# The MLP's up projection by seven block products instead of eight, with all block sums of weights built in device memory

## The chip, the cores and the metric

The kernel runs on one core of a Trainium2 chip. The metric is device time in microseconds. The kernel before takes 828.75 us, the median of three runs (828.61 to 828.80). The engines are named as in the profile: PE is TensorE (matrix products; PEld its weight loads), DVE is VectorE, ACT is ScalarE, POOL is GpSimd, SP is SyncE, which here only issues transfers.

## The reference

One encoder layer over x of 512 tokens by 1024, in float32. A token mixer (two kinds of recurrent heads, both directions) and a cross-attention add to x; then comes the part that is changed, a squared-ReLU MLP with 4096 hidden columns, and a final RMSNorm:

```python
def squared_relu_mlp(xn, w_up, w_down):
    return jnp.square(jax.nn.relu(xn @ w_up)) @ w_down

x = x + squared_relu_mlp(rmsnorm(x, norm_mlp[l]), w_up[l], w_down[l])
```

## The kernel before

**Precision.** Every large product runs as three passes: each operand is split into a rounded part (`hi`, made by ScalarE as a copy) and the rest (`lo`, made by VectorE as a subtraction), and hi·hi, hi·lo and lo·hi are added in PSUM (`split_out`, `mm3`).

**Weights.** The host packs the weights into blocks of 128 by 1024 (`wpk`, 512 KB each) in the order of their use. `load` brings a block to an `st` tile on SP's queue (three buffers), `split` makes its `wh` and `wl` (three buffers each); `weights` keeps splits up to two blocks and loads three blocks ahead, at raised priority.

**Stages.** First the input projections with the recurrent heads interleaved as generators (`tick`), then the memory projections, `out`, the query projection `xq` with the attention heads, the attention's output projection `xo`, and then for f = 0 to 3 an up stage (1024 hidden columns) and a down stage of the MLP.

**Products by seven.** `xo` and the four down stages already use a scheme with seven instead of eight block products (P1 to P7): the token halves and the weight blocks are combined by sums, the seven products accumulate in three PSUM banks per token tile (`by_blocks`), and VectorE adds them to the residual `xr`. Sums of weight blocks (names T2, U, T3) are made by `sum_loads` and `add_block`: POOL issues a plain load into SBUF, and then loads that add on arrival. Each product and half g is one "job" with one weight tile; `ahead` splits the tiles up to two jobs ahead.

**Up before.** `proj_d` runs 8 output blocks of 128 columns, each over 8 blocks of the contraction, three passes, 512 tokens wide. The transposed x (`x3T`, made by `turn_two`) is not yet normalised; the row of factors 1/rms (`rrow`) is multiplied in on the result together with the ReLU, so that the first up blocks (`first_two`) run before the norm is known. ScalarE squares, and VectorE and ScalarE make the sums and splits (`e["P1"]` to `e["P7"]`) for the down stage.

**Order.** TensorE's order in the last stages is the program's order. ScalarE, VectorE and the queues are put in order ahead of time by a planner: each engine takes, of what the plan has ready, what stands earliest in the program; `tc.high_priority()` moves a piece ahead. `behind(a, b)` puts a after b on an engine.

Of the kernel before, what the change touches and what calls it, by code (L numbers as in the profile page):

```python
# [10 lines left out]
F32 = mybir.dt.float32  # L11
# [34 lines left out]
def _split_order():  # L46
# [18 lines left out]
    for f in range(4):  # L65
        for j in range(4):
            seq += d("up", 1024 * f + P * j, 1) + d("up", 1024 * f + P * (j + 4), 1)
        seq += [("t", "down", 8 * f + 2 * g + k, 0) for g in range(2) for k in (0, 4)]
        seq += [("t", "down", 8 * f + 2 * g + 4, 512) for g in range(2)]
# [7 lines left out]
NSTREAM = len(SEQ) - 10  # L77
# [3 lines left out]
def trunk(ctx: ExitStack, tc: tile.TileContext, x, mem, wpk, vec, cst, lmask, rmask, rows, out):  # L81
    nc = tc.nc
    big = ctx.enter_context(tc.tile_pool(name="big", bufs=1))
    sb = ctx.enter_context(tc.tile_pool(name="sb", bufs=1))
    psm = ctx.enter_context(tc.tile_pool(name="psm", bufs=4, space=PSUM))
# [163 lines left out]
    def weights(key):  # L249
        i = SIDX[key]  # L250
        with (tc.high_priority() if i > 2 else ExitStack()):
            for n in range(i, i + 3):
                split(n)
            load(i + 3)
        return hl_tiles[i]

# [819 lines left out]
    ORDER = ("P1", "P2", "P6", "P5", "P7", "P3", "P4")  # L1076
    LATE = [(p, g) for p in ORDER[2:] for g in range(2)]
    JOBS = {f: [("P1", 0), ("P2", 0), ("P1", 1), ("P2", 1)] + LATE for f in range(4)}

    JOBS[-1] = [(p, g) for p in ("P1", "P7", "P2", "P5", "P6", "P3", "P4") for g in range(2)]  # L1080
# [5 lines left out]
    def sum_loads(f, names):  # L1086

        parts = {"T2": ((0, 1), (1, 1), (0, 0)), "U": ((0, 1), (0, 0)), "T3": ((0, 1), (1, 1))}
        for nme in names:
            if nme == "T3":  # L1090
                t2 = [G4()[:, :] for _ in range(2)]
            else:
                t = A16()
                t2 = [t[:, g * 1024:g * 1024 + 1024] for g in range(2)]
            for g in range(2):
                sums[f, nme, g] = t2[g]
        return [add_block(sums[f, nme, g], block(f, g, *parts[nme][i]), i > 0)
                for i in range(3) for nme in names for g in range(2) if i < len(parts[nme])]
# [6 lines left out]
    SUMS = {f: {"P6": "T2", "P5": "U", "P7": "T3", "P4": "T2"} for f in range(4)}  # L1105
    SUMS[-1] = {"P6": "T3", "P5": "U", "P7": "T3", "P4": "T3"}

    def job(f, n):

        if n >= len(JOBS[f]):  # L1110
            if f < 3:
                split(SIDX["d", "up", 0, 1024 * (f + 1)] + n - len(JOBS[f]))
            return None
        p, g = JOBS[f][n]
        if p in PLAIN:
            i = block(f, g, *PLAIN[p])
            split(i)
            return hl_tiles[i]
        if (f, n) not in jobs_hl:
# [343 lines left out]
```

## Time and profile before

| | |
|---|---|
| median of 3 runs | 828.75 us |
| profiled execution | 828.9 us, span 826.9 us |
| granted TensorE clock | 0.998 |
| PE / PEld / DVE / ACT / POOL busy | 98% / 82% / 71% / 52% / 9% |
| DMA | 118.9 MB, mean 144 GB/s |
| `xo`'s end and up stage 0 | 485.4 to 536.5 us |
| down stages f = 0 to 3 | start at 536.5, 618.1, 699.7, 781.3 us, 38.1 us each |
| up stages f = 1 to 3 | start at 574.6, 656.2, 737.8 us, 43.5 us each |

The span runs from the first to the last instruction; the profiled execution's own time has 2.0 us around it. Busy time of matmuls is modelled from their starts: a matmul of 512 columns is listed with 0.39 us though the next one starts 0.23 us after it. Lines named L258 are those of the helper `split_out`; L261 to L263 are `mm3`, L1153 to L1155 the products of `by_blocks`, L1102 POOL's transfers, L236 the weight loads.

### The profile page before, as it was taken

The numbers are of one execution on the slowest core, as the hardware profiler recorded it, in microseconds if no ns is written. First come the engines' busy times: TensorE is split into PE (matmuls) and PEld (weight loads), VectorE is DVE, ScalarE is ACT, GpSimd is POOL, SyncE is SP. The second block draws the span as 40 slices with busy tenths as digits, with TensorE's granted clock in tenths as the row PEclk, the third lists the DMA queues.
The fourth block names the chain that finished last, engine by engine and source line by source line (L and its number), as shares of the span: only waits on it lengthen the run. The fifth ranks groups of instructions, "written<-read, shape, count | busy, mean of one in ns | idle before, by whom it ended". The sixth has DMA issues, their size and how long they took to land.

```text
span 826.9 us, 12625 instructions
## 1 busy us (share of the span) xinstructions
PE 813.4 (98%) x4862; PEld 676.1 (82%) x4862; DVE 590.9 (71%) x1046; ACT 431.9 (52%) x771; POOL 77.7 (9%) x131
## 2 busy tenths in 40 slices
PE   8999999999999999999999999999999999999996
PEld 6788778877878988887888888888888888888885
DVE  6568975699479898545668985676668566756685
ACT  5247564545578485345455675443454345434544
POOL 2000000100010000100100004022102210211001
PEclk9999999999999999999999999999999999999999
DMA  7332223322342334532343349969836982798332
GB/s 277 118 120 91 78 79 106 100 89 79 102 128 78 128 128 154 151 98 83 111 119 76 81 128 302 254 171 275 217 102 182 280 211 91 189 290 207 110 70 101
DMA packets 34125, 118.91 MB, mean 144 GB/s; under 512 B 3921, under 2 KB 4049, under 8 KB 34066
## 3 DMA queue, kind: packets, MB, share of 16 engines
q1 hardware_dynamic: 22832, 77.80, 27.5%
q0 software_dynamic: 10944, 39.85, 21.8%
q8 instruction: 38, 0.62, 0.3%
q10 hardware_dynamic: 290, 0.47, 0.1%
q14 instruction: 21, 0.17, 0.1%
HBM read 116.00 MB, written 2.10 MB: 143 GB/s over the span
## 4 chain that ended last, share of the span: by engine, by line
PE 84%; issue 6%; DVE 6%; ACT 2%; DMA 1%; POOL 1%; POOLq 0%; ACTq 0%; DVEq 0%
PE mm L261 17%; PE mm L263 17%; PE mm L262 17%; PE sm L1153 6%; PE sm L1155 6%; PE sm L1154 6%; PE mm L1153 2%; PE mm L1155 2%; PE mm L1154 2%; DVE wl L258 2%; PE sm L827 1%; PE sm L562 1%; PE sm L486 1%; ACT wh L258 1%; DVE t L759 1%
## 5 line engine op out<-in xcount | busy, mean ns | idle before, releaser
L258 ACT ACTIVATE wh<-st 128x1024 fp32r<-128x1024 f32 x131 | 138.7, 1060 | 185.2 <-PE mm L262 117.9
L261 PE MATMUL mm<-xT,wh 128*128 128x512 f32 x544 | 215.3, 396 | 0.0
L258 DVE TENSOR_TENSOR wl<-st,wh 128x1024 fp32r<-128x1024 f32 x131 | 160.1, 1223 | 76.1 <-ACT wh L258 75.6
L263 PE MATMUL mm<-xT,wl 128*128 128x512 f32 x544 | 212.8, 391 | 0.1
L262 PE MATMUL mm<-xT,wh 128*128 128x512 f32 x544 | 212.4, 390 | 0.3 <-DVE xT L975 0.3
L263 PEld LDWEIGHTS mm<-xT,wl 128*128 128x128 f32 x544 | 102.1, 188 | 21.9 <-DVE wl L258 0.3
L262 PEld LDWEIGHTS mm<-xT,wh 128*128 128x128 f32 x544 | 102.3, 188 | 20.8 <-DVE xT L975 0.9
L261 PEld LDWEIGHTS mm<-xT,wh 128*128 128x128 f32 x544 | 102.2, 188 | 20.7 <-ACT wh L258 0.3
L1102 POOL DMA_DIRECT2D as<-in_wpk x52 | 39.6, 763 | 250.2 <-DVE wl L258 162.0
L1342 DVE SCALAR_TENSOR_TENSOR t<-mm,rg 128x512 f32<-128x512 f32 x32 | 22.0, 691 | 52.1 <-PE mm L263 52.0
L1153 PE MATMUL sm<-wh,yT 128*128 128x512 f32 x128 | 49.8, 389 | 0.0
L1154 PE MATMUL sm<-wl,yT 128*128 128x512 f32 x128 | 49.8, 389 | 0.0
L1155 PE MATMUL sm<-wh,yT 128*128 128x512 f32 x128 | 49.8, 389 | 0.0
L258 ACT ACTIVATE wh<-as 128x1024 fp32r<-128x1024 f32 x26 | 27.6, 1062 | 37.0 <-PE sm L1155 23.7
L258 DVE TENSOR_TENSOR wl<-as,wh 128x1024 fp32r<-128x1024 f32 x26 | 31.9, 1226 | 14.0 <-ACT wh L258 14.0
L1153 PE MATMUL sm<-wh,a 128*128 128x512 f32 x84 | 32.9, 391 | 0.0
L1155 PE MATMUL sm<-wh,a 128*128 128x512 f32 x84 | 32.7, 389 | 0.0
L1154 PE MATMUL sm<-wl,a 128*128 128x512 f32 x84 | 32.7, 389 | 0.0
L1285 DVE TENSOR_TENSOR vv<-vv,sm 128x512 f32<-128x512 f32 x48 | 31.0, 681 | 1.7 <-PE sm L1155 1.7
L199 POOL TENSOR_TENSOR tiny<-tiny,misc 128x4 f32<-128x4 f32 (+1 forms) x10 | 9.6, 963 | 201.3 <-DVE tiny L197 136.2
L1155 PEld LDWEIGHTS sm<-wh,yT 128*128 128x128 f32 x128 | 24.0, 188 | 5.0
L1154 PEld LDWEIGHTS sm<-wl,yT 128*128 128x128 f32 x128 | 24.0, 188 | 5.0
(329 smaller groups left out, 1566.8 us busy)
## 6 DMA issues: line engine op xcount, KB each, us to landing
st<-in_wpk SPq DMA_DIRECT2D x131, 512.0 KB, 3.4
as<-in_wpk POOLq DMA_DIRECT2D x52, 512.0 KB, 6.9
gate<-in_wpk POOLq DMA_DIRECT2D x24, 512.0 KB, 7.1
as<-in_x SPq DMA_DIRECT2D x4, 512.0 KB, 6.8
vv<-in_x SPq DMA_DIRECT2D x8, 256.0 KB, 4.0
out<-vv SPq DMA_DIRECT2D x7, 256.0 KB, 2.2
a<-in_mem SPq DMA_DIRECT2D x2, 512.0 KB, 3.7
t<-in_rows SPq DMA_DIRECT2D x2, 256.0 KB, 5.3
```

The costliest lines, as they stand in the source:

```text
L199: gp.tensor_tensor(out=r, in0=ms, in1=nh.to_broadcast([P, w]), op=ALU.pow)
L258: return sc.activation(dst_hi, src, AF.Copy), v.tensor_tensor(out=dst_lo, in0=src, in1=dst_hi.bitcast(F32), op=ALU.subtract)
L261: pe.matmul(ps, lhsT=ah, rhs=bh, start=first, stop=False)
L262: pe.matmul(ps, lhsT=ah, rhs=bl, start=False, stop=False)
L263: pe.matmul(ps, lhsT=al, rhs=bh, start=False, stop=last)
L486: mm = pe.matmul(ps[b * i:b * i + b, z:z + b], lhsT=kc[j][:, w * P + b * i:w * P + b * i + b], rhs=rhs(j, w * P, i), start=True, stop=True)
L1102: return gp.dma_start(out=dst, in_=wpk[idx], **kw)
L1153: pe.matmul(ps, lhsT=ah, rhs=bh, start=new, stop=False, **fl)
L1154: pe.matmul(ps, lhsT=ah, rhs=bl, start=False, stop=False, **fl)
L1155: pe.matmul(ps, lhsT=al, rhs=bh, start=False, stop=end and k == 1, **fl)
L1285: added = v.tensor_tensor(out=z, in0=z, in1=ps, op=ALU.add if sign > 0 else ALU.subtract)
L1342: v.scalar_tensor_tensor(out=y, in0=ps, scalar=0.0, in1=rrow[:, 0:512], op0=ALU.max, op1=ALU.mult)
```

## The change

**Up by seven products.** The new function `up(st)` splits the 1024 by 1024 up product of a stage into blocks of halves: contraction, hidden columns and tokens. Each half g of 256 hidden columns in a block has seven products, 14 jobs a stage, in an order written out in `MORDER`. A job is 2 output tiles by 4 contraction blocks by 3 passes, 256 tokens wide. P1, P6, P7 and P4 add up in one PSUM bank A, P5 and P3 in a bank C, P2 in a bank B; the bank is read out between the products, and `first` to `fourth` make the sums that the down stage needs from the squared results.

**The normalised x.** The products combine halves of x, so these are multiplied by 1/rms beforehand: `flip` transposes and scales by the gain, `rstd_half` and `norm_half` make the factors of one token half, multiply, combine and split. `after_product` puts their TensorE parts between the products. `first_two`, `turn_two` and `rms_row` go.

**Weights.** For each of the eight MLP stages (up and down) and each g the four sums P5, P7, P6 and P4 are built in device memory by `make_forms`: SP fills a form from a weight block or copies one from another form, POOL adds a weight block to it. One or two steps are issued at each `weights` call from the fifth block on, the rest at every third MLP job. In the MLP each job, form or plain block, is one load on SP (`mload`), three to six jobs ahead; the splits stay up to two jobs ahead (`msplit`). The loads with sums into SBUF remain for `xo` alone. The down stages' order of products becomes P1, P5, P2, P6, P3, P7, P4, g by g.

```diff
-NSTREAM = len(SEQ) - 10
+NSTREAM = SIDX["d", "up", 0, 0]
...
+        for _ in range(0 if i < 4 else 1 + i % 2):
+            next(form_steps, None)
         return hl_tiles[i]
...
+            for g in range(2):
+                for p in ("P5", "P7"):
+                    yield lambda: mfill(nc.sync, f[p, g][:, :], st, g, (0, 1))
+            for g in range(2):
+                yield lambda: mfill(gp, f["P5", g][:, :], st, g, (0, 0), True)
+                yield lambda: mfill(gp, f["P7", g][:, :], st, g, (1, 1), True)
+            for src, dst, b in (("P7", "P6", (0, 0)), ("P6", "P4", (1, 0))):
+                for g in range(2):
+                    yield lambda: nc.sync.dma_start(out=f[dst, g][:, :], in_=f[src, g][:, :], max_dma_last_dim=4096)
+                for g in range(2):
+                    yield lambda: mfill(gp, f[dst, g][:, :], st, g, b, True)
+
+        for s0 in range(0, 8, 2):
+            for a, b in zip(steps(s0), steps(s0 + 1)):
+                a()
+                yield 1
+                b()
+                yield 1
...
+    MORDER = [seq("1a 2a 1b 2b 5a 5b 3a 6a 3b 7a 6b 4a 7b 4b")] + [two("P1", "P5", "P2", "P6", "P3", "P7", "P4"),
+              seq("1a 2a 5a 1b 3a 5b 6a 2b 7a 6b 4a 3b 7b 4b")] * 4
...
+    def mahead(n):
+        with tc.high_priority():
+            for m in range(n, n + 3):
+                msplit(m)
+            for m in range(n + 3, n + 7):
+                mload(m)
+        if n % 3 == 0:
+            next(form_steps, None)
+        return mhl[n]
...
+    def norm_half(u):
+
+        ps = smb()
+        for t in range(2):
+            pe.transpose(ps[:, t * P:t * P + P], rt[u][:, t:t + 1].to_broadcast([P, P]), ident)
+        with tc.high_priority():
+            sc.activation(rrow[:, u * 256:u * 256 + 256], ps[:, 0:256], AF.Copy)
+            for p, x in ((("P1", fx[0, 0]), ("P2", fx[0, 1])) if u == 0 else (("P5", sraw[0]),)):
+                for h in range(2):
+                    times_r(x, u, h)
+                    part_split(p, x, h)
+        if u == 0:
+            return
+        d = sraw[0]
+        x1, x3_, x2_, x4 = fx[0, 0], fx[0, 1], fx[1, 0], fx[1, 1]
+        v.tensor_tensor(out=d, in0=d, in1=x1, op=ALU.subtract)
+        v.tensor_tensor(out=x3_, in0=x3_, in1=d, op=ALU.add)
+        split_out(*xf["P3"], x3_)
+        split_out(*xf["P6"], d)
+        for h in range(2):
+            times_r(x2_, 1, h)
+        v.tensor_tensor(out=x1, in0=x1, in1=x2_, op=ALU.subtract)
+        split_out(*xf["P7"], x1)
+        for h in range(2):
+            times_r(x4, 1, h)
+        split_out(*xf["P4"], x4)
...
+    def up(st):
...
+        def square(t, src):
+            sc.activation(t, src, AF.Relu)
+            sc.activation(t, t, AF.Square)
...
+        def first(g):
+            v.tensor_tensor(out=y[3, g], in0=y[2, g], in1=y[3, g], op=ALU.subtract)
+            form("P5", g, y[3, g], A4)
+        def second(g):
+            v.tensor_tensor(out=y[3, g], in0=y[3, g], in1=y[0, g], op=ALU.subtract)
+            form("P6", g, y[3, g], A4)
...
+        for n, (p, g) in enumerate(MORDER[st]):
+            hi, lo = mahead(len(JOBS) * st + n)
...
+            ps = B[g] if p == "P2" else C[g] if p in ("P5", "P3") else A[g]
+            xh, xl = xf[p]
+            for k in range(2):
+                o = ps[:, k * 256:k * 256 + 256]
+                for kt in range(4):
+                    z = slice(k * 512 + kt * P, k * 512 + kt * P + P)
+                    m = slice(kt * 256, kt * 256 + 256)
+                    new = k == kt == 0 and p in ("P1", "P2", "P5")
+                    pe.matmul(o, lhsT=hi[:, z], rhs=xh[:, m], start=new, stop=False, **fl)
+                    pe.matmul(o, lhsT=hi[:, z], rhs=xl[:, m], start=False, stop=False, **fl)
+                    pe.matmul(o, lhsT=lo[:, z], rhs=xh[:, m], start=False, stop=kt == 3, **fl)
+                after_product()
...
+            if p == "P7":
+                v.tensor_tensor(out=y[3, g], in0=y[3, g], in1=ps, op=ALU.subtract)
+                square(y[3, g], y[3, g])
+                form("P4", g, y[3, g], A4)
+            elif p == "P4":
+                y[2, g] = T2()[:, 0:512]
+                square(y[2, g], ps)
+                first(g)
+                if g == 0:
+                    second(g)
+                    third(g)
+                    fourth(g)
```

More of the change, by code (lines that the diff above doesn't have):

```diff
@@ L1104, in trunk, with job @@
     PLAIN = {"P1": (0, 0), "P2": (1, 0), "P3": (1, 1)}
[L1105 to L1114, printed above, removed]
+    SUMS = {"P6": "T3", "P5": "U", "P7": "T3", "P4": "T3"}
+    def job(n):
+        if n >= len(JOBS):
+            return msplit(n - len(JOBS))
+        p, g = JOBS[n]
@@ L1125, in job @@
                     behind(a, b)
-            jobs_hl[f, n] = (hi, lo)
-            if f < 0 and p == "P7":
-                add_block(s_, block(f, g, 0, 0))
+            jobs_hl[n] = (hi, lo)
+            if p == "P7":
+                add_block(s_, block(-1, g, 0, 0))
             if p == "P6":
-                add_block(s_, block(f, g, 1, 0))
-        return jobs_hl[f, n]
+                add_block(s_, block(-1, g, 1, 0))
+        return jobs_hl[n]
+    two = lambda *ps: [(p, g) for p in ps for g in range(2)]
@@ new lines, in trunk, with mload @@
+    seq = lambda s: [("P" + w[0], "ab".index(w[1])) for w in s.split()]
+    MORDER = [seq("1a 2a 1b 2b 5a 5b 3a 6a 3b 7a 6b 4a 7b 4b")] + [two("P1", "P5", "P2", "P6", "P3", "P7", "P4"),
+              seq("1a 2a 5a 1b 3a 5b 6a 2b 7a 6b 4a 3b 7b 4b")] * 4
+    MJ = [(st, p, g) for st in range(8) for p, g in MORDER[st]]
+    mst, mhl, msum = {}, {}, []
+    def mload(n):
+        if n < len(MJ) and n not in mst:
+            st, p, g = MJ[n]
+            mst[n] = T("st", 1024, 3)
+            if p in PLAIN:
+                mfill(nc.sync, mst[n][:, :], st, g, PLAIN[p])
+            else:
+                nc.sync.dma_start(out=mst[n], in_=mforms[st, p, g][:, :], max_dma_last_dim=4096)
@@ L1218, in heads_in, with after_product @@
             drain()
+    later = []
+    def after_product():
+        for w in list(later):
+            w[0] -= 1
+            if w[0] < 0:
+                later.remove(w)
+                w[1]()
+    fx, rt, sraw = {}, {}, [None]
     def add_out(t, c, ps, sign, last):
         z = xr[t, c]
-        last_add[0] = v.tensor_tensor(out=z, in0=z, in1=ps, op=ALU.add if sign > 0 else ALU.subtract)
-        if last:
+        v.tensor_tensor(out=z, in0=z, in1=ps, op=ALU.add if sign > 0 else ALU.subtract)
+        if not last:
+            return
+        with (tc.high_priority() if (t, c) in ((1, 1), (3, 0)) else ExitStack()):
@@ L1303, in add_to @@
         finish(t, r, pieces[t])
-    def first_two():
-        i0 = SIDX["d", "up", 0, 0]
-        for j in range(2):
-            split(i0 + j)
-        w = [hl_tiles[i0 + j] for j in range(2)]
-        for j in range(2, 5):
-            load(i0 + j)
-        two = [mmb(), mmb()]
-        for half in (4, 0):
-            for j in range(2):
-                for k in range(half, half + 4):
-                    z = slice(k * P, k * P + P)
-                    mm3(two[j], w[j][0][:, z], w[j][1][:, z], x3[k][0], x3[k][1], k == 4, k == 3)
-                    if whole and j == 0 and k == 7:
-                        turn_two(*whole.pop(0)[1:])
-                        with tc.high_priority():
-                            behind(split(i0 + 2), last_add[0])
-        rms_row()
-        return two
```

285 lines of the change are left out of this document (174 added, 111 removed).

## The prediction

> **What bounds the kernel now.** I read the page's engine table and chain first, then who waits on TensorE, then TensorE, VectorE and ScalarE by MLP stage. The first rows are the page's:
>
> ```profile
> span 826.9 us, 12625 instructions
> PE 813.4 (98%) x4862; PEld 676.1 (82%) x4862; DVE 590.9 (71%) x1046; ACT 431.9 (52%) x771; POOL 77.7 (9%) x131
> PE 84%; issue 6%; DVE 6%; ACT 2%; DMA 1%; POOL 1%; POOLq 0%; ACTq 0%; DVEq 0%
> ```
>
> The waits of TensorE, longest and last:
>
> ```profile
> PE sm L349 <- DMA cs<-in_cst: 1.3, 1, 1.3
> ...
> PE mm L262 <- DVE wl L258: 0.2, 1, 0.2
> ```
>
> Seven such rows sum to 5.7 us, none in the MLP. So TensorE's instruction stream sets the time, and time can only be lost if it is made to wait. The stretches (columns: length, then busy time of PE, PEld, DVE, ACT, POOL, clock, DMA share, GB/s) are the first 465 us, the seam from the output projection into the MLP, and one up and one down stage:
>
> ```profile
> 20.70:485.40 464.70, 461.66 (x3296) 386.03 (x3296) 344.49 (x692) 259.70 (x532) 21.58 (x41) 1.00 0.35 105
> 485.40:536.54 51.14, 51.14 (x237) 42.46 (x236) 34.54 (x58) 28.11 (x50) 11.16 (x15) 1.00 0.87 245
> 574.62:618.14 43.52, 43.52 (x193) 36.04 (x192) 27.59 (x42) 19.57 (x29) 3.47 (x4) 1.00 0.64 191
> 618.14:656.22 38.08, 38.08 (x169) 31.53 (x168) 27.60 (x35) 17.04 (x18) 8.51 (x12) 1.00 0.78 195
> ```
>
> An up stage is 192 matmuls in 43.52 us, 0.2267 us each; a down stage 168 in 38.08, the same pace. TensorE is gapless; VectorE is at 63% and 72%, ScalarE at 45%.
>
> **Up by seven products: the gain.** Each up stage becomes 14 block products of 24 matmuls, 336 in all, each 256 columns wide. This width stands in the memory projection; the timeline has 22 of them in a row:
>
> ```profile
> 274.71 0.28 PE L263 MATMUL mm<-a,wl 128*128 128x256 f32 x1
> ...
> 277.23 0.28 PE L263 MATMUL mm<-a,wl 128*128 128x256 f32 x1
> ```
>
> 21 steps in 2.52 us: 0.120 us each, not half of 0.2267 (0.113). So 336 x 0.120 = 40.3 against 43.5: 3.2 us a stage, **12.8 us over four**, 1.5%. If halving were exact it would be 21.8; the row excludes that. A product takes 2.88 us.
>
> The Trainium skill's "TensorE: Matmul & The Clock Gate", section "Back-to-back issue gap", gives N/2.4 + 2.5 ns when warm, so 216 and 109 ns, and by it the four stages would save 18.9 us (an estimate from that page). This trace has 227 and 120 ns, 11 ns more on each, so the trace disagrees and decides: more but narrower matmuls pay that extra 144 times more per stage.
>
> **What VectorE and ScalarE get to do.** Rows of one seam up to down, in time order, ScalarE then VectorE:
>
> ```profile
> 618.12 1.06 ACT L258 ACTIVATE wh<-st 128x1024 fp32r<-128x1024 f32 x1 [3.40 <-PE mm L262]
> 619.08 0.62 ACT L1343 ACTIVATE t<-t 128x512 f32<-128x512 f32 x1
> 622.03 1.14 ACT L258 ACTIVATE yT<-t 128x512 fp32r<-128x512 f32 x2
> ```
>
> ```profile
> 618.34 0.69 DVE L1342 SCALAR_TENSOR_TENSOR t<-mm,rg 128x512 f32<-128x512 f32 x1 [3.01 <-PE mm L263]
> 619.21 1.23 DVE L258 TENSOR_TENSOR wl<-st,wh 128x1024 fp32r<-128x1024 f32 x1 [0.17 <-ACT wh L258]
> 620.35 0.42 DVE L1358 TENSOR_TENSOR t<-t,t 128x256 f32<-128x256 f32 x1
> 620.69 0.68 DVE L258 TENSOR_TENSOR a<-t,a 128x512 fp32r<-128x512 f32 x1
> 621.29 0.42 DVE L1359 TENSOR_TENSOR t<-t,t 128x256 f32<-128x256 f32 x1
> 621.63 0.42 DVE L1360 TENSOR_TENSOR t<-t 128x256 f32<-128x256 f32 x1
> 621.96 0.42 DVE L1361 TENSOR_TENSOR t<-t,t 128x256 f32<-128x256 f32 x1
> 622.30 1.22 DVE L258 TENSOR_TENSOR wl<-st,wh 128x1024 fp32r<-128x1024 f32 x1
> 623.43 1.28 DVE L258 TENSOR_TENSOR yT<-t,yT 128x512 fp32r<-128x512 f32 x2
> ```
>
> Start to start in a full queue, a weight split costs ScalarE 0.96 (618.12 to 619.08) and VectorE 1.13 (622.30 to 623.43); a 512-wide operation costs about 0.57 and 0.60 (620.69 to 621.29). An up stage now has 14 weight splits instead of 8; per half g three bank copies, four squarings of two ScalarE operations each, three subtractions or adds from a bank, and sums and splits for its forms, 11 splits and 5 sums of them within the stage. ScalarE: 14 x 0.96 + (6 + 16 + 11) x 0.57 = 32 us of 40.3 (80%). VectorE: 14 x 1.13 + (6 + 5 + 11) x 0.60 = 29 us (72%). That fits on average. What counts is where TensorE waits for one of these.
>
> **Place one, 7b to 4b.** P1, P6, P7 and P4 accumulate in one bank per g, each read out before the next writes. Everywhere in the orders another product lies between, 2.88 us of cover, except at "7b 4b": 4b may not start until VectorE has subtracted bank A of 7b. With VectorE free that is 0.16 (a matmul's tail, 0.28 less 0.12) + 0.68 + hand-overs of about 0.05: 0.9 us. But 4a ended two products earlier, and releases a chain for g=0: two squarings, then four sums and four splits (VectorE 8 x 0.60), which stand earlier in the program than 7b's subtraction. Beside them lie the sum and split from 3b (1.2) and three weight splits at raised priority (3.4). The sums partly serialise, since the second rewrites in place what P5's split still reads. 9.4 us of VectorE work thus stands ahead of the subtraction, begins about 1.2 us after 4a and has 5.8 us until 7b ends: 1.2 + 9.4 - 5.8 = 4.8 us late. VectorE's order is fixed ahead of the run; that the earlier instruction in the program wins when ready is seen at 620.69, where the split of a (earlier in the code) goes ahead of L1359 to L1361, and at 622.30, where the raised weight split overtakes yT. Bounds 0.9 and 5.9 (with idle gaps while it waits for ScalarE); near the serial case I take **4.0 us, three times: +12**.
>
> **Place two, the seam into up(0).** Before, the first up blocks ran on raw x while the normalisation caught up: 485.40 to 536.54 is gapless. Now the normalised x must be multiplied by r, combined and split before each product. VectorE: P1 and P2 8 x 0.60, P5 6 x 0.60, the rest 2 x 1.2 (scalings) + 7 x 1.13 = 10.3; 18.7 us on top of 29, against 40.3 plus some 3 us of lead. ScalarE: transposed copies and splits, some 12 us on 32. Up to the third pair (3a, 17.3 us into the stage) VectorE owes 23 us of raised splits, adds and forms in about 24 us, with idle gaps while r goes through POOL:
>
> ```profile
> L1261 POOL TENSOR_TENSOR tiny<-tiny,misc 128x4 f32<-128x4 f32 x1 | 1.0, 1032 | 21.0 <-DVE tiny L981 21.0
> ...
> L955 ACT ACTIVATE t<-vv 128x512 f32<-128x512 f32 x24 | 15.0, 626 | 10.3 <-DVE vv L961 5.9 <-DVE vv L1285 3.1 <-DVE vv L1222 1.2
> ...
> L1285 DVE TENSOR_TENSOR vv<-vv,sm 128x512 f32<-128x512 f32 x48 | 31.0, 681 | 1.7 <-PE sm L1155 1.7
> ```
>
> The chain add 0.68, square 0.8 (0.63 and reading its sum), two small steps 0.3, this power 1.0, broadcast 0.4, scale 0.6, split 1.3 is 5 us; cover is the last product of the output projection (5.4 us with its transposes). So P1a and P2a start 0.5 to 1.5 us late, P3 1 to 2, and at "4a 7b 4b", with one product of cover less than later, 7b's subtraction comes 1 to 6 late. Bounds 2 and 12; I take **+7**. The transposes themselves are as many as before.
>
> **Forms in device memory.** Removed: 64 POOL loads into SBUF in the MLP; no TensorE wait named one, so 0. Added: 64 fills and copies on SP's queue, 64 accumulates on POOL's; 97 of the 128 within the 65 weight fetches before the output projection, the rest in the MLP.
>
> ```profile
> q1 hardware_dynamic: 22832, 77.80, 27.5%
> q0 software_dynamic: 10944, 39.85, 21.8%
> st<-in_wpk SPq DMA_DIRECT2D x131, 512.0 KB, 3.4
> as<-in_wpk POOLq DMA_DIRECT2D x52, 512.0 KB, 6.9
> SPq L236 <- DVE wl L258: 483.3, 83, 18.5
> ```
>
> A plain 0.52 MB takes the 16 engines 1.5 us (227 us for 77.8 MB), one of q0's 76 transfers 2.4 on average (180/76). 97 steps at 1.5 to 2.9 us are 145 to 280 us in 465, on a DMA share of 0.35: 0.66 to 0.95. Copies memory to memory stand in no row; a copy waits for an accumulate's landing, and SP's weight loads queue behind it, as POOL's powers do behind an accumulate. But SP already sits waiting for a free buffer 483 us in all: loads run two blocks (11 us) ahead of need, more than 6.9, and each copy comes four steps (over 15 us) behind what it needs. Bounds 0 and +8 (one wait of under 0.1 us per step); I take 0. In the MLP one 0.5 MB load per 2.8 us is 187 GB/s, below 245 reached. The end (P3 now ahead of P7, then P4) is the same length.
>
> Sum: 828.9 (span 826.9 + 2.0 around it; median of the runs 828.75) - 12.8 + 12 + 7 + 0 = **835**.
>
> **Rivals.** *VectorE keeps up* (0.40): 7b's subtraction fits into a gap while VectorE waits for ScalarE, as the 3.0 us idle ahead of 618.34 shows it has gaps today; up(0) loses 3. 828.9 - 12.8 + 3 x 1.1 + 3 = 822. For it: averages of 72 to 80%. Against: the burst sits just there.
>
> *The seams cost little, but the early stages slow down* (0.11): copies on SP meet late accumulates, weight loads come after their need, and TensorE waits where it now waits 5.7 us in all. 822 + 8 to 20: 830 to 842. It decides once a load lands more than 11 us after its slot came free. This is also how the change would not do what it says: forms not ahead of their stage.
>
> *The clock drops* (0.07): after each gap of 4 to 6 us matmuls restart at a lower clock. Here no gap exceeds 1.3 us and the granted clock is 1.00 in every stretch, so no row prices it: 0 at least; if each of four gaps were followed by half pace for as long as the gap itself, 4.5 us, that is 4 x 2.25 = 9 us on the forecast, 844. The Trainium skill's "TensorE: Matmul & The Clock Gate", section "Why this matters for your kernels", asks for no idle gap over about 3 us, or the clock falls back to half; no run here shows it yet.
>
> **Numbers.** Forecast 0.42 (own range 830 to 842), rivals as given. Under 820 or over 846 about 0.15 stays out, so 820 to 846. 0.2%, about what can be told from no change, is 1.7 us. Faster 0.39 (nearly all of the first rival), within 0.2% 0.09, slower 0.52 (the forecast, the clock, most of the second rival).
>
> **What would show it.** Up stages at 336 matmuls with 0.120 us steps; TensorE waits "<- DVE" at the subtraction of P7's bank, three or four of 3 to 5 us, and several around the first up stage; VectorE's queue full there; no waits for weight splits before 480 us. Wrong if those waits are about 1 us (then 822), or if TensorE waits for DMA or weight splits in the early stages.

## The result and the profile after

The changed kernel takes 995.4 us (median of four runs, 994.2 to 998.5) against 828.8 for the kernel before: 1.202 times, interval 1.199 to 1.204. The forecast was 835, its range 820 to 846. The sign was right; 166.6 us were lost where 6.1 were forecast.

The page of the kernel after, its first rows, the clock and DMA slices (40 equal slices of 24.8 us, in tenths), POOL's queue and the longest TensorE waits by place:

```profile
span 993.7 us, 14157 instructions
PE 841.6 (85%) x5438; PEld 722.5 (73%) x5438; DVE 622.1 (63%) x1033; ACT 486.1 (49%) x854; POOL 90.7 (9%) x132
PEclk9985987967597899999999999899999999999998
DMA  9999999999999234334432534245455455465543
q0 software_dynamic: 15040, 39.85, 21.4%
```

```profile
PE sm L647 <- DVE t L640: 26.1, 3, 25.1
PE sm L532 <- DVE a L623: 24.3, 5, 9.3
PE sm L724 <- DVE a L721: 18.7, 1, 18.7
PE sm L588 <- ACT as L580: 18.4, 2, 11.2
PE sm L1497 <- ACT a L304: 16.7, 3, 5.6
```

Four of these five rows lie in the recurrent heads, long before the MLP; before, seven waits summed to 5.7 us. The DMA engines are full for the first 13 slices, and in these the clock is at its lowest (digit 5 in two of them). The stretches of the kernel after (length, then busy time of PE, PEld, DVE, ACT, POOL, clock, DMA share, GB/s):

```profile
20.70:100.00 79.30, 54.16 (x218) 42.60 (x216) 31.77 (x76) 19.45 (x26) 16.90 (x24) 0.81 1.04 274
100.00:200.00 100.00, 76.59 (x760) 60.94 (x760) 47.45 (x88) 35.21 (x55) 20.93 (x24) 0.89 1.06 276
200.00:300.00 100.00, 49.56 (x392) 41.48 (x393) 30.87 (x51) 23.34 (x50) 22.41 (x27) 0.71 1.05 269
300.00:400.00 100.00, 84.59 (x684) 68.94 (x683) 68.81 (x122) 54.25 (x117) 8.38 (x22) 0.91 0.46 128
```

The table gives the stages, read from the timelines as the start of the first matmul of each, in us. The time is the median of the runs; the stages are of the one profiled execution (for e15 its fastest, 829.2). Rows after the second are experiments, told below.

| kernel | time | up f=0 starts | up f=0 | down f=0 | up f=1 | down f=1 |
|---|---|---|---|---|---|---|
| before | 828.8 | 491.6 | 44.9 | 38.1 | 43.5 | 38.1 |
| after | 995.4 | 632.3 | 49.5 | 43.4 | 48.0 | 38.7 |
| e2, no forms | 853.3 | 492.7 | 49.1 | 43.4 | 47.8 | 38.8 |
| e3, and subtraction first | 836.1 | 492.5 | 49.1 | 43.4 | 42.0 | 38.8 |
| e11, and 7b 4a 4b | 835.0 | 492.2 | 48.5 | 43.5 | 40.3 | 40.4 |
| e12, and P2 ahead of P5 | 826.5 | 492.4 | 48.3 | 38.8 | 40.3 | 38.8 |
| e15, all of it with forms | 831.8 | 494.0 | 48.4 | 38.8 | 40.3 | 38.7 |

So the 166.6 us fall into two parts: 140.7 are lost before the MLP begins (632.3 against 491.6), and the other 25.9 after that.

**Ahead of the MLP.** The rows of the form transfers in the kernel after (accumulates, fills, copies: durations of the issue, then first and last start), and of the weight loads issued from 60 to 300 us with the time to their landing:

```profile
L273 POOL DMA_DIRECT2D form_P<-in_wpk x64: 827/1036/1211, 18.1 to 312.5; - x64
L273 SPq DMA_DIRECT2D form_P<-in_wpk x32: 490/597/3691, 12.5 to 255.1; - x32
L290 SPq DMA_DIRECT2D form_P<-form_P x32: 469/470/482, 34.1 to 303.6; - x32
...
L237 SPq DMA_DIRECT2D st<-in_wpk x19: 333/540/1996, 68.0 to 284.5; - x19
DMA to landing us min/median/max: 8.2/12.4/26.4
```

All 128 are gone by 312 us, also the 31 that the program issues in the MLP. Nothing held them to their place: a fill depends on nothing, so the planner, which gives an idle queue whatever is ready, put them ahead. The weight loads came late. The first 28 of them, in the kernel after up to 303.6 us:

```profile
L237 SPq DMA_DIRECT2D st<-in_wpk x28: 328/524/1996, 1.2 to 284.5; - x28
```

The first 28 of the kernel before, and its loads from 60 to 300 us with their landing:

```profile
L236 SPq DMA_DIRECT2D st<-in_wpk x28: 327/328/493, 1.2 to 155.0; - x28
...
L236 SPq DMA_DIRECT2D st<-in_wpk x38: 327/328/336, 60.2 to 299.7; - x38
DMA to landing us min/median/max: 3.0/3.3/4.2
```

The 28th was issued at 284.5 instead of 155.0 us, 129.5 later. From 60 to 300 us there were 19 loads where 38 had been, and one took 12.4 us to land instead of 3.3. Up to 320 us ScalarE waited 14 times, 121.6 us in all, to split a block that had not landed:

```profile
ACT wh L304 <- DMA st<-in_wpk: 121.6, 14, 15.6
```

The longest wait of TensorE came another way. The factor 1/rms of a recurrent head is a power on POOL; what it needs is ready at 238.7 us, but seven accumulates stand ahead of it on POOL's queue, and each of them waits for a transfer to land:

```profile
270.44 1.04 POOL L273 DMA_DIRECT2D form_P<-in_wpk  x1 [7.06 <-DMA form_P<-in_wpk]
271.02 1.53 POOL L200 TENSOR_TENSOR tiny<-tiny,misc 128x4 f32<-128x4 f32 x1
272.59 0.69 DVE L640 TENSOR_TENSOR t<-t,tiny 128x512 f32<-128x512 f32 x1 [33.89 <-POOL tiny L200]
273.43 1.09 PE L647 MATMUL sm<-cs,t 128*128 128x128 f32 x4 [25.08 <-DVE t L640]
```

In the 18.7 us of L724 the last 5.3 are of the same kind: VectorE waits for a memset on POOL behind an accumulate. By these rows some 30 of the 140.7 us come through POOL's queue, and the rest, as far as rows show it, through late weight loads and the clock behind the waits. No run takes POOL's steps alone out of that queue.

**In the MLP.** TensorE's first matmul of 4b in up f=1 and VectorE's queue ahead of it:

```profile
768.43 0.55 PE L1497 MATMUL sm<-xT,wh 128*128 128x256 f32 x1 [5.58 <-ACT a L304]
```

```profile
762.84 0.69 DVE L1469 TENSOR_TENSOR t<-t,as 128x512 f32<-128x512 f32 x1
...
764.05 0.68 DVE L1473 TENSOR_TENSOR rg<-rg,t 128x512 f32<-128x512 f32 x1
764.66 1.22 DVE L304 TENSOR_TENSOR wl<-st,wh 128x1024 fp32r<-128x1024 f32 x1
...
767.00 0.68 DVE L1477 TENSOR_TENSOR as<-as,t 128x512 f32<-128x512 f32 x1
767.60 0.68 DVE L1520 TENSOR_TENSOR t<-t,sm 128x512 f32<-128x512 f32 x1
```

L1469, L1473 and L1477 are `second`, `third` and `fourth` of half 0; L1520 is the subtraction from P7's bank. It ends at 768.28 and TensorE starts at 768.43. The releaser that the row names (a form's split on ScalarE) is not the one: raised in e3, the subtraction takes most of the gap away. After the gap comes the clock:

```profile
768.40:772.00 3.60, 3.57 (x17) 3.60 (x18) 1.36 (x2) 1.81 (x3) 0.00 (x0) 0.50 0.11 40
```

### The profile page after: what moved, and what is told of

Its sections match the earlier page's. It is cut to its first block, busy times and chain, and to the rows that moved or that the text cites. A ratio compares the mean times of both kernels' runs of the same rounds, so it can differ in the third digit from the quotient of the medians.

```text
span 993.7 us, 14157 instructions
## 1 busy us (share of the span) xinstructions
PE 841.6 (85%) x5438; PEld 722.5 (73%) x5438; DVE 622.1 (63%) x1033; ACT 486.1 (49%) x854; POOL 90.7 (9%) x132
## 3 DMA queue, kind: packets, MB, share of 16 engines
q0 software_dynamic: 15040, 39.85, 21.4%
## 5 line engine op out<-in xcount | busy, mean ns | idle before, releaser
L304 DVE TENSOR_TENSOR wl<-st,wh 128x1024 fp32r<-128x1024 f32 x187 | 228.6, 1223 | 214.2 <-ACT wh L304 213.1
L304 ACT ACTIVATE wh<-st 128x1024 fp32r<-128x1024 f32 x187 | 197.6, 1058 | 308.0 <-DMA st<-in_wpk 122.3
L307 PE MATMUL mm<-xT,wh 128*128 128x512 f32 x288 | 121.7, 424 | 0.0
L308 PE MATMUL mm<-xT,wh 128*128 128x512 f32 x288 | 117.5, 408 | 0.3 <-DVE xT L1021 0.3
L309 PE MATMUL mm<-xT,wl 128*128 128x512 f32 x288 | 117.7, 409 | 0.1
L273 POOL DMA_DIRECT2D form_P<-in_wpk x64 | 60.4, 945 | 232.6 <-DMA form_P<-form_P 123.8
L1229 PE MATMUL sm<-wh,a 128*128 128x512 f32 x180 | 71.1, 395 | 2.8 <-ACT a L304 1.7
L1231 PE MATMUL sm<-wh,a 128*128 128x512 f32 x180 | 70.9, 394 | 0.8 <-DVE a L304 0.8
L307 PEld LDWEIGHTS mm<-xT,wh 128*128 128x128 f32 x288 | 57.8, 201 | 11.9 <-ACT wh L304 0.3
L308 PEld LDWEIGHTS mm<-xT,wh 128*128 128x128 f32 x288 | 57.7, 200 | 11.9 <-DVE xT L1021 0.9
L1497 PE MATMUL sm<-xT,wh 128*128 128x256 f32 x128 | 40.2, 314 | 17.9 <-ACT a L304 16.7
L1229 PEld LDWEIGHTS sm<-wh,a 128*128 128x128 f32 x180 | 34.0, 189 | 11.5 <-issue 2.6
L1497 PEld LDWEIGHTS sm<-xT,wh 128*128 128x128 f32 x128 | 27.7, 217 | 19.0 <-ACT a L304 17.2
L1498 PE MATMUL sm<-xT,wh 128*128 128x256 f32 x128 | 39.4, 308 | 1.3 <-DVE xT L304 1.2
L1231 PEld LDWEIGHTS sm<-wh,a 128*128 128x128 f32 x180 | 34.1, 189 | 8.4 <-DVE a L304 1.3
L1497 PE MATMUL mm<-xT,wh 128*128 128x256 f32 x128 | 36.8, 287 | 0.0
L1498 PE MATMUL mm<-xT,wh 128*128 128x256 f32 x128 | 36.6, 286 | 0.0
## 6 DMA issues: line engine op xcount, KB each, us to landing
form_P<-in_wpk SPq DMA_DIRECT2D x32, 512.0 KB, 17.2
```

Of the source, the lines that this page charges most:

```text
L273: return eng.dma_start(out=dst, in_=mblock(st, g, *b), max_dma_last_dim=4096, **kw)
L304: return sc.activation(dst_hi, src, AF.Copy), v.tensor_tensor(out=dst_lo, in0=src, in1=dst_hi.bitcast(F32), op=ALU.subtract)
L307: pe.matmul(ps, lhsT=ah, rhs=bh, start=first, stop=False)
L308: pe.matmul(ps, lhsT=ah, rhs=bl, start=False, stop=False)
L309: pe.matmul(ps, lhsT=al, rhs=bh, start=False, stop=last)
L1229: pe.matmul(ps, lhsT=ah, rhs=bh, start=new, stop=False, **fl)
```

## Experiments: what takes the early time

**e1, transfers held to their place.** A fill or copy may not pass the weight load ahead of it in the program; nothing else changes.

```diff
-        nc.sync.dma_start(out=t, in_=wpk[i])
+        last_load[0] = nc.sync.dma_start(out=t, in_=wpk[i])
...
-                    yield lambda: mfill(nc.sync, f[p, g][:, :], st, g, (0, 1))
+                    yield lambda: in_place(0, mfill(nc.sync, f[p, g][:, :], st, g, (0, 1)))   # behind(..., last_load[0])
```

> The kernel after, with each fill and copy of a form held on SP's queue behind the weight load that stands ahead of it in the program (same transfers, same number, spread over the stages). Theory 'pulled ahead': the loss of 141 us before the MLP comes from all 128 form transfers being issued in the first 312 us, three to each weight load, so that the DMA engines are full and the weight loads land late; spread, the output projection ends at 490 to 500 us as before and the time is 850 to 860 us (828.8 + the 26 us lost in the MLP). Rival 'volume': the transfers cost the same wherever they stand, since copies wait for accumulates and block SP's queue: 940 to 995 us.

Measured 887.6 us (885.1 to 890.0). Of the 142 us that the kernel after takes over e2 (below), three quarters are gone with the same bytes moved, so volume alone is not the cause; but the MLP still starts 26.7 us later than in e2, which neither theory had. POOL's accumulates are not held here, and 16.3 us of the 26.7 are waits of TensorE that come through POOL, as above: 9.4 us at L652 for the power (L647 above; 1.1 us in e2) and 6.9 at L729 for the memset (L724 above).

**e5 and e6, half the forms; no accumulates.** Both unheld, as in the kernel after.

```diff
-        for s0 in range(0, 8, 2):
+        for s0 in range(0, 4, 2):          # e5; stages 4 to 7 read plain blocks
...
+        if accumulate:                     # e6, in mfill
+            return None
```

> The kernel after with forms for MLP stages 0 to 3 alone (64 transfers instead of 128, nothing holds them to their place); stages 4 to 7 read a plain block in place of each form, so the sums of those weights are left out. Theory (the transfers are pulled ahead and crowd the weight loads): in the kernel after about three transfers of 2.3 us of engine time stand for each of the first 42 weight loads, so a block takes 1.5 + 3 x 2.3 = 8.4 us where TensorE needs one per 5.5; 42 x 2.9 = 122 of the 141 us lost ahead of the MLP. With half the transfers at the same density the crowd lasts for about 21 loads: 21 x 2.9 = 61 us, plus the 853 of the kernel without forms: 905 to 930 us, and TensorE undisturbed from about 200 us on. Rival (what counts is the volume against what the engines have free over the whole stretch): 64 x 2.3 = 147 us on a share of 0.35 of 465 us fits easily, so 853 to 862.

> The kernel after with the 64 accumulates on POOL's queue left out (so the forms are not sums); the 64 fills and copies on SP's queue stay where they are, pulled ahead as before. Theory (engine time per weight load): 1.5 + 1.5 x 1.6 = 3.9 us per block, under the 5.5 that TensorE needs, so nearly nothing is lost ahead of the MLP: 853 to 868 us. Rival (it is SP's queue: weight loads stand behind 64 transfers, and copies wait there, whatever POOL adds): most of the 141 us stay, over 930 us. Between the two: the copies' place on SP counts with a part.

Measured 904.6 (904.5 to 904.8) and 854.0 (853.1 to 854.9). With half the transfers TensorE is undisturbed again from 200 us on. From 100 to 300 us in e5:

```profile
100.00:200.00 100.00, 88.27 (x844) 72.04 (x843) 59.38 (x111) 47.06 (x86) 14.65 (x19) 0.91 0.87 235
200.00:300.00 100.00, 98.63 (x928) 80.25 (x927) 77.38 (x134) 56.60 (x117) 6.95 (x19) 1.00 0.30 93
```

Without accumulates the forms cost 0.7 us over e2, although SP's 64 fills and copies are as free as before, all issued by 200 us. This takes away both the accumulates' time on the engines and what stood behind them on POOL. The first stretch of e6, and its row of POOL's queue:

```profile
20.70:100.00 79.30, 79.11 (x602) 63.34 (x600) 58.50 (x123) 39.15 (x53) 0.16 (x2) 1.00 0.90 309
```

```profile
q0 software_dynamic: 1728, 6.29, 3.5%
```

POOL's queue took 21.4% of 993.7 us of the engines in the kernel after and 3.5% of 851.3 in e6: 213 and 30 us, so 64 accumulates took 183, 2.9 us each, twice a plain load.

**e9, the transfers alone.** The kernel before with the first 97 transfers issued at the same weight fetches and read by nobody.

```diff
         return hl_tiles[i]   # in weights() of the kernel before
+        for _ in range(0 if i < 4 or i > 68 else 1 + i % 2):
+            next(form_steps, None)
```

> The kernel before, its up projection by eight blocks and its MLP untouched, with the first 97 form transfers of the change added at the same weight fetches, pulled ahead by the planner in the same way; nothing reads the forms (and the halves of an up block are taken from whole blocks, so the sums are not those of the change). Theory (the transfers alone take the early time, whatever the MLP does): 97/128 of the 141 us, 107, plus 829: 920 to 950 us, with TensorE undisturbed once they have landed. Rival (the loss needs the new up projection, its longer residual stage or the forms being read): under 845.

Measured 917.4 (916.1 to 918.7): 88.5 us lost in a kernel whose MLP is untouched. Over their bases the loss is 51 us for 64 transfers (e5 less e2), 88 for 97, 142 for 128 (after less e2): it grows with the number, a little faster than in proportion. The times of e5 and e9 lie just under what was expected (905 to 930 and 920 to 950).

**e17, the wait of SP's queue.** In the kernel after SP stands at copies whose accumulate has not landed:

```profile
SPq L237 <- DVE wl L304: 216.3, 41, 17.6
SPq L290 <- DMA form_P<-in_wpk: 171.9, 34, 15.6
```

```diff
-                    yield lambda: nc.sync.dma_start(out=f[dst, g][:, :], in_=f[src, g][:, :], max_dma_last_dim=4096)
+                    yield lambda: mfill(nc.sync, f[dst, g][:, :], st, g, (0, 1))
```

> The kernel after with one edit: the 32 transfers on SP's queue that copy one form into another read a plain weight block instead (so these forms start from the wrong block and the sums are wrong). Their number, bytes, place in SP's queue and POOL's 64 accumulates stay, pulled ahead as before; only SP's wait at a copy for an accumulate that has not landed, 171.9 us in 34 waits in the kernel after, is gone. Theory A (SP's queue is in order: weight loads stand behind a copy that waits for an accumulate): most of the 141 us ahead of the MLP goes, and the time is 855 to 900. Theory B (the engines' time is what is short: 128 transfers at about 2.3 us each within some 300 us, whoever waits): at least two thirds stay, 950 to 1000.

Measured 983.0 (982.7 to 983.3): theory B. Without most of that wait the time is 12 of the 167 us shorter, though 74.1 us of waiting at form transfers remain on SP in this run. VectorE's longest wait for the power on POOL stays too, 36.6 us instead of 33.9. The weight loads of e17 from 60 to 300 us show why little came of it:

```profile
L237 SPq DMA_DIRECT2D st<-in_wpk x19: 328/334/3295, 66.7 to 291.1; - x19
DMA to landing us min/median/max: 8.9/22.9/30.0
```

As many loads as in the kernel after, 19; what they no longer wait at SP, they wait behind the other transfers once issued (22.9 us to landing instead of 12.4).

## Experiments: what the MLP costs

These leave the sums of weights out: each form is replaced by a plain block, with the same loads in the MLP and no transfers to build it.

**e2 and e3, no forms; the subtraction first.**

```diff
-    form_steps = make_forms()
+    form_steps = iter(())
...
+                with tc.high_priority():   # e3, in up()
                     v.tensor_tensor(out=y[3, g], in0=y[3, g], in1=ps, op=ALU.subtract)
```

> The kernel after without any form in device memory: each job that needs a sum reads a plain weight block of the same size in its place, so the sums of weights are left out of the computation. Both theories of the early loss: the output projection ends at 491 us as before, time 851 to 857 us, which prices the new up stages and the seam alone at +23 to +28 us. If something else of the change slows the early stages (program size, the buffers), it stays above 900.

> As the run without forms, and VectorE's subtraction from the bank of P7 at raised priority. Theory 'queue': 4b starts 5.6 us late in three up stages since that subtraction stands behind the sums and splits released by 4a, and each gap is followed by some 4 us at half the granted clock (2 us more). Raised, the gap is about 1 us and the clock stays: three times 6.5 us less, 832 to 838 us. Rival: the row names ScalarE's split as the releaser, so 4b waits for that or for its weights and not for the subtraction: no change, 851 to 857 us.

Measured 853.3 (851.8 to 854.8) and 836.1 (832.7 to 836.2), both as expected. The priority thus takes 17.2 us of place one away, 5.7 three times: gap, and clock behind it. What is left in e3 is still the same wait:

```profile
622.59 0.69 DVE L1469 TENSOR_TENSOR t<-t,as 128x512 f32<-128x512 f32 x1
623.20 0.68 DVE L1521 TENSOR_TENSOR t<-t,sm 128x512 f32<-128x512 f32 x1
```

```profile
624.02 0.35 PE L1497 MATMUL sm<-xT,wh 128*128 128x256 f32 x1 [1.43 <-ACT wh L304]
```

L1521 is the subtraction. VectorE had just begun another operation as 7b ended (622.60), so the subtraction ends at 623.88 and TensorE starts 0.14 us later, as it does in the kernel after (0.15). The weight split that the row names is not the releaser: TensorE began to load the weights of this matmul at 623.99, before a split that ends at 624.01 could have made them.

**e8, P5's form of half 1 first in stage 0.** `square`, `first(1)` of up f=0 at raised priority, on e3.

> No forms (plain blocks in their place, sums of weights left out), subtraction from P7's bank at raised priority, and in up stage 0 the last squaring and P5's sum and split of half 1 at raised priority too. The first down stage took 43.4 us against 38.1 because its second product on P5 waited behind VectorE's and ScalarE's backlog and the clock fell after it. If that backlog is only a matter of order, the stage falls to 38.5 to 40.5 us and the time to 831 to 834. Rival (VectorE is simply behind by the normalisation's work, so another operation is late in its place): 835 to 838.

Measured 836.3 (832.0 to 836.5), and down f=0 at 43.4 as before: the time is the rival's. VectorE was busy for 43.7 of the 49.7 us of up f=0 there, and priority alone won nothing.

**e11 and e12, the orders of products.** On e3.

```diff
-seq("1a 2a 5a 1b 3a 5b 6a 2b 7a 6b 4a 3b 7b 4b")
+seq("1a 2a 5a 1b 3a 5b 6a 2b 7a 6b 3b 7b 4a 4b")   # e11
...
-two("P1", "P5", "P2", "P6", "P3", "P7", "P4")
+two("P1", "P2", "P5", "P6", "P3", "P7", "P4")      # e12, with second and third hung on (P2, 0) and (P5, 0)
```

> No forms (plain blocks in their place, sums of weights left out), subtraction from P7's bank at raised priority, and in up stages 1 to 3 the order ends 6b 3b 7b 4a 4b instead of 6b 4a 3b 7b 4b, so that product 4a (2.88 us) lies between 7b and 4b. If TensorE's remaining wait there (1.4 us, three times) is the subtraction's cover, the stages fall from 42.0 to about 40.6 us and the time from 836 to 831 to 833. Rival (4b waits for its own weight split, which stands behind other work on ScalarE whatever lies between): 835 to 838.

> As the run with the order 7b 4a 4b (no forms, plain blocks in their place, sums of weights left out), and in the down stages P2 goes ahead of P5, which gives P5's sum and split two more products of 2.7 us. That run had the up stages at 40.3 us, the full gain, and the wait back in the next down stage (1.4 us ahead of P5 of half 1, 0.8 ahead of another product, three times over). If the wait is a matter of cover, a pair of up and down falls from 80.7 to 79 us or less and the time from 835 to 829 to 832: then all that is left over the kernel before is the seam out of the output projection. Rival (ScalarE and VectorE stay behind by the same work, and another form is late in its turn): 833 to 836.

Measured 835.0 (834.7 to 835.2) and 826.5 (824.6 to 827.6). e11 met its time only by the rival, but not by the rival's mechanism: the up stage did fall to 40.3 us, as it should if the last 1.4 us were the subtraction's missing cover, and the down stage behind it rose by 1.7. The wait had moved to P5 of half 1, 1.42 us from start to start of these two matmuls of e11, instead of 0.23:

```profile
633.23 0.40 PE L1230 MATMUL sm<-wl,a 128*128 128x512 f32 x1
...
634.65 0.50 PE L1231 MATMUL sm<-wh,a 128*128 128x512 f32 x1 [1.02 <-DVE a L304]
```

e12 gives that form two more products of cover. Up f=1 and the down stage behind it in e12:

```profile
579.49:619.81 40.32, 40.32 (x338) 40.31 (x337) 26.43 (x29) 28.77 (x40) 0.00 (x0) 1.00 0.58 183
619.81:658.57 38.76, 38.38 (x170) 31.47 (x169) 33.00 (x44) 20.43 (x24) 0.00 (x0) 1.00 0.59 190
```

Gapless in up, 0.4 us of idle in down, and down f=0 went from 43.5 to 38.8 too, so that the time lies under the 829 to 832 expected. With forms for nothing, the change is then worth 0.3% (ratio 0.9970, 0.9960 to 0.9981).

## Experiments: can the forms be had for nothing

In these nothing is left out.

**e4, e7, e10, e13: pace.** e4 is e1 with the subtraction first. e7, e10 and e13 also hold POOL's accumulates to their place and issue no step in the memory's key and value projection; e7 has 85 transfers ahead of the MLP (the expectation of e10 says 86) and one at every second job in it, and the priorities of e8; e10 has 98 and one at every third job, e13 adds e12's orders to e10.

```diff
-        for _ in range(0 if i < 4 else 1 + i % 2):
+        for _ in range(0 if i < 4 or 37 <= i < 53 else 2):   # e10; e7: 1 + (i % 4 > 0)
```

> The paced kernel with the subtraction raised as well, nothing left out. If both theories hold, their gains add: 832 to 841 us. If the seam is the larger part of the 26 us, 845 to 855 us; if the transfers slow the early stages even when spread, 5 to 20 us more than the same without forms.

> Nothing is left out. Fills, copies and also POOL's accumulates are each held behind the weight load that stands ahead of them in the program; no step at the 16 fetches of the memory's key and value projection, seven per four fetches elsewhere, the rest at every second MLP job; the subtraction from P7's bank at raised priority, and in up stage 0 the last squaring and P5's sum and split of half 1 as well. If the early loss is a matter of pace alone, at most 10 of the 34 us of the paced kernel remain, and the MLP is that of the kernel without forms and with the subtraction first (836) less 2 to 4 at the first down stage: 832 to 846. Rival (128 transfers cost some 30 us at any pace, because a share over about 0.75 delays some weight load somewhere): 860 to 872.

> Nothing is left out. As in the run with transfers spread, but two steps at each weight fetch outside the memory's key and value projection (98 ahead of the MLP instead of 86) and one at every third MLP job as in the kernel after, instead of every second; subtraction from P7's bank at raised priority, no other priority changed. If the MLP's 30 us over the kernel without forms came from the step at every second job, it falls to about 10 (as in the paced kernel, whose MLP takes 352 us against 342), and with 10 to 20 ahead of the MLP the time is 855 to 867. Rival (every place that is given less only hands the loss to another): 868 to 880.

> Nothing is left out: the run with the forms spread ahead of the MLP (853.8), with the two orders of products that took the kernel without forms from 836 to 826.5 (7b 4a 4b in up, P2 ahead of P5 in down). If the costs of place one and of the forms are independent terms, 853.8 - 9.6 = 844, so 841 to 847. Rival (the MLP's form transfers make weight splits late there, and the orders free nothing): 849 to 855.

Measured 873.3 (870.0 to 876.5), 872.1 (870.9 to 876.3), 853.8 (852.5 to 855.1) and 846.1 (845.2 to 847.8). e4 missed: held to their place the transfers cost 37 us over e3, not the 5 to 20 expected. Its MLP starts at 522.7 us against 492.5 in e3, and waits through POOL make up most of that (13.9 us at L652, 6.9 at L729). With the accumulates held, in e7 and e10, these fall to 1.1 us at L652 and at most 1.3 at L729. e7 missed as well: its MLP starts at 503.0, but takes 371.5 us to the span's end against e4's 352.0, so what was won early was lost later. e10 kept the early gain and gave the MLP back its pace, 1 us better than expected; e13 won 7.7 of the 9.6 us expected from the orders.

In e10 almost all the early loss is one row, a wait for a scan whose mask is a load of 128 KB. Its issue, and the scan's start on VectorE:

```profile
55.80 0.66 SPq L734 DMA_DIRECT2D a<-in_rmask  x1
```

```profile
73.84 1.21 DVE L752 TENSOR_TENSOR_SCAN a<-a,a 4x512 f32<-4x512 f32 x1 [11.91 <-DMA a<-in_rmask]
```

It took 18 us behind the first forms.

**e14, e15, e16: a later start, all ahead, the rest in down.** On e13: transfers begin at the tenth weight block and run at one step per fetch through the key and value projection, the mask's load at raised priority (104 ahead of the MLP; which of the two edits does it is not separated); e15 takes two and three in turn elsewhere (126 ahead); e16 moves the last 24 of e14 into later stages.

```diff
-        for _ in range(0 if i < 4 or 37 <= i < 53 else 2):
+        for _ in range(0 if i < 9 else 1 if 37 <= i < 53 else 2):   # e14; e15: 2 + i % 2
...
+        with tc.high_priority():
             nc.sync.dma_start(out=rm[0:64, 0:512], in_=rmask)
```

> As that one, but the transfers begin at the tenth weight block instead of the fifth (two per fetch, one in the key and value projection; 104 ahead of the MLP), and the load of the row mask, which the scan of the first heads waits for, is at raised priority. In the run with the forms spread, nearly the whole loss ahead of the MLP is one wait of 10.0 us for that scan, whose mask of 128 KB was issued at 55.8 us and came by 73.8 us behind the first forms. If what is left of the early loss is this one small load, the MLP starts at 492 to 495 us instead of 503.5 and the time is 831 to 838. Rival (it is the volume: the accumulates then disturb another place as much): 841 to 847, no better than the run beside it.

> Nothing is left out: the run with the later start, but two and three steps in turn at the weight fetches outside the key and value projection, so that 126 of 128 transfers stand ahead of the MLP. The later-start kernel begins its MLP at 491.6 us, as the kernel before does, with 104 transfers ahead of it; what it loses against the kernel without forms (826.5) is in the MLP, 12 us, mostly up stages 0 and 1, where 24 transfers are left. If the stretch ahead of the MLP has room for these too, the time falls to 826 to 830. Rival (the share ahead of the MLP is at its limit, 0.93 of the DMA engines from 100 to 200 us): weight loads come late there again, 838 to 855.

> Nothing is left out: the later-start kernel with its last 24 transfers taken out of up stage 0 and put mostly into the down stages (every second job there, every seventh of up stages 1 and 2). If the 12 us against the kernel without forms come from transfers in the up stages, where a stage's work on ScalarE and VectorE is densest, up stage 0 falls from 53.2 to 48.4 us and the time to 828 to 833. Rival (any transfer beside the MLP's own loads makes a split late): 835 to 840.

Measured 838.5 (835.9 to 840.6), 831.8 (829.2 to 835.3) and 838.1 (838.0 to 838.4). e14 lies half a us above the range expected and e15 1.8 above its own; e16 lies in its rival's. e14's MLP starts at 491.6 us, as in the kernel before: 104 transfers cost nothing there. e15 puts nearly all of them ahead and still starts it at 494.0, with the stages of e12. e15 from 100 to 200 us, and its weight loads in the same stretch:

```profile
100.00:200.00 100.00, 99.51 (x1102) 80.91 (x1102) 79.65 (x140) 51.13 (x95) 21.91 (x30) 1.00 1.05 290
```

```profile
L242 SPq DMA_DIRECT2D st<-in_wpk x14: 327/333/540, 110.6 to 195.7; - x14
...
DMA to landing us min/median/max: 5.5/10.0/12.7
```

This narrows what e17 showed. The DMA share is that of the kernel after in the same 100 us (1.05 and 1.06), but 14 weight loads were issued there, as many as in the kernel before, against 8, and TensorE did 1102 matmuls against 760. The form transfers issued were 38 against 44, so 2.7 to a weight load against 5.5. Full engines alone cost next to nothing; what costs is how many transfers stand ahead of the next load, or the next step of POOL, that TensorE needs.

e16 is no faster than e14, and its edit did not do all it should: nine of POOL's instructions, 8.4 us, still lie in its up f=0 (three, 2.6 us, in e15), so this stage stayed at 53.2 us. Behind it the cost moved with the transfers: up f=1 fell from 44.6 to 40.3 us, and down f=1 rose from 38.8 to 44.4, where ScalarE waited for the load of a form and TensorE 3.7 us a little later, as the rival had it:

```profile
654.59 1.06 ACT L309 ACTIVATE wh<-st 128x1024 fp32r<-128x1024 f32 x1 [3.96 <-DMA st<-form_P]
```

In all, 22 transfers beside the MLP's own loads cost 7 us (e14 less e15).

No kernel with everything in it beats the kernel before: e15 is 1.0035 times it (1.0022 to 1.0049).

## Why the prediction was wrong

**The step that failed** is "Forms in device memory", and in it one premise: "97 of the 128 within the 65 weight fetches before the output projection". The places in the program were taken for times of issue. All 128 were issued in the first 312 us, and the share was not "0.66 to 0.95" over 465 us but 1.04 to 1.06 from 20.7 to 300. The sentence after it, that "each copy comes four steps (over 15 us) behind what it needs", rests on the same premise and fell with it. "Bounds 0 and +8" should have been bounds on two cases: placed as written, and placed as early as their dependences allow. The second was there to be worked out: 128 transfers at the predicted 1.5 to 2.9 us are 190 to 370 us of engine time, and the weight loads of those 300 us come behind them. The prediction also had "as POOL's powers do behind an accumulate": one such wait alone measured 25.1 us of TensorE, where the whole term was bounded by 8. The row read as cover, "SPq L236 <- DVE wl L258: 483.3", was the opening: an idle queue is where a planner puts what is ready.

**The price of a transfer** was right: 2.9 us for an accumulate is the end of the predicted 1.5 to 2.9. So was the value 0, under another placement (e14; in e15 the MLP starts 1.7 us later than in e12).

**The rival on the early stages** had the mechanism (loads that "come after their need", deciding "once a load lands more than 11 us after its slot came free": 12.4 us from issue alone, at the median, here), with 0.11 and a price of 8 to 20 us. It sized the copies' waits on SP, which e17 shows to be minor, not the weight loads queued behind the rest, nor POOL's own steps.

**The gain of up by seven** was right: steps of 0.120 us, and 40.3 us for an up stage in e11, e12 and e15, the 40.3 predicted. (The 18.9 us that the prediction estimates beside this should be 19.0; nothing hangs on it.)

**Place one** was right in kind and place: P7's bank, behind the chain from 4a. The term was 4.0 and measured 5.6 of gap, near its bound of 5.9; the rest of an up stage's 47.8 us in e2 (40.3 + 5.6 leaves 1.9) is the clock. Three times 7.5 instead of 4.0 are 10.5 us of the sum. Priority took 5.7 of each 7.5 away (e2 less e3) and the order of e11 the rest. The lower bound of 0.9 was a little small: raised, the wait is 1.43 us, since VectorE had just begun another operation.

**The clock** had a rival of its own, "half pace for as long as the gap itself". At 0.50 right behind a gap of 5.58 us that was the right size, 2.25 predicted and 1.9 measured (the row shows 0.50 for 3.6 us, not for as long as the gap), but it belonged in the forecast as soon as that assumed gaps of 4 us. The rule of the Trainium skill's "TensorE: Matmul & The Clock Gate", section "Why this matters for your kernels", that no idle gap should be over about 3 us, agrees with this row; another row, below, does not fit it.

**Place two** was +7, so up f=0 was to take 44.9 - 3.2 + 7 = 48.7 us; it takes 49.1 in e2. That is luck in part. TensorE's five waits there (1.2, 1.0, 0.8, 0.4 and 0.4 us) sum to 3.8, and the one at 4b is 0.8 where 1 to 6 were predicted; much of the rest is the clock, which the term left out: 0.70 over the first 7.6 us of the stage, 0.93 over the whole. What was missed lies behind it: down f=0 at 43.4 instead of 38.1, as VectorE and ScalarE still owed P5's form. That is 5.3 us in e2, and all but 0.7 of it is gone in e12 by order.

**The sum** without forms was to be 835 and was 853.3 (e2). Of the 18 us missed, 10.5 are place one with its clock, 5.3 the first down stage, the rest small. It adds up; the 142 us of the forms then stand on top.

## What to carry to other kernels

A transfer that depends on nothing is issued when the scheduler finds its queue idle, not where the program has it: cost it once at its place and once at the earliest place that its dependences allow, and tie it behind a load if the second is dear. What counts for a load that is needed on time is how many transfers are queued ahead of it, not how full the engines are on average; and a queue that issues waiting transfers and also computes makes the computing late. A wait taken away from a busy engine's work can reappear at the next operation with the least cover (e11). Priority was worth 17.2 us where the operation only stood behind others (e3) and nothing in e8; there the order of products gave the cover (e12). Where several things are waited for, the releaser that a row names can be the wrong one: see whether that operation ended just before the wait did, as was done for 4b.

## What the runs showed of the hardware that was not expected

**Full engines without loss.** A mean DMA share of 1.05 over 100 us left TensorE at 99.5% (e15; 99.5% in the kernel before), with weight loads landing 10.0 us after issue instead of 3.3.

**The clock falls without a long gap.** In the kernel after, early in up f=0, the longest idle of TensorE was 1.21 us, yet the granted clock went to 0.50:

```profile
632.30:637.00 4.70, 2.59 (x15) 1.67 (x13) 4.70 (x7) 2.33 (x5) 0.00 (x0) 0.92 0.43 129
637.00:642.00 5.00, 4.57 (x22) 4.57 (x23) 2.72 (x6) 3.77 (x9) 0.69 (x1) 0.50 0.25 88
```

TensorE was busy 2.59 of 4.70 us, 55%, in short pieces. A limit on single gaps does not cover that. The Trainium skill's "TensorE: Matmul & The Clock Gate", section "What's actually happening", says that the gate follows how busy TensorE was in a recent window of some 3.4 us; this row fits that better than the gap rule, though no run here shows which share is too little.

**An accumulate costs twice a load.** 2.9 us of the 16 engines for 0.5 MB added to device memory (the kernel after less e6), against 1.5 for a plain load of the same size.
